# Lane pacing in a fused decoder layer: longer waits in the weight joining, a staging tile for the second output projection, and earlier loads of the norm's gains

## The chip, the cores and the metric

The kernel runs on one core of one Trainium2 chip. A core has several engines that run side by side, each with its own queue of instructions in order: TensorE (PE: matrix products; its weight loads are shown as PEld), VectorE (DVE), ScalarE (ACT), GpSimd (POOL), and SyncE (SP), which here does nothing but issue transfers. Transfers run on 16 DMA engines. The metric is the device time of one execution in microseconds (us); lower is better. Before the change three runs took 1999.65 to 2007.75 us, with a median of 2001.74 us.

## What is computed

One decoder layer on an input x of 2048 rows and 1024 columns, all in float32:

```python
hn = rms_norm(h, mix_pre_g)
proj = hn @ w_in                       # 1024 -> 1792: q, k, v, u
attn_out = sliding_window_attention(q, k, v, attn_sinks, rel_bias)
conv_out = conformer_conv(u, conv_dw, ..., w_conv_pw)
mixed = concatenate([attn_out, conv_out]) @ w_out
h = h + rms_norm(mixed, mix_post_g)
hn = rms_norm(h, ffn_pre_g)
f = (silu(hn @ w_gate) * (hn @ w_up)) @ w_down        # 1024 -> 2816 -> 1024
h = h + rms_norm(f, ffn_post_g)
```

Attention looks 128 positions back. The convolution group is a gated unit, a depthwise convolution with 31 taps, a norm, a swish and a pointwise product with `w_conv_pw`.

## The kernel before

**Precision.** A float32 value is split in a high part, in a format that TensorE takes at full speed, and the low rest, and each product is the sum of three matmuls (`three`, line 108 issues them): high by high, high by low, low by high. A split is an ACT copy for the high part and a subtraction for the low one. `split_w` (lines 128 to 138) does this for weights, with the copy on ACT at line 133 and the subtraction on POOL at line 135 when it takes place beside the early stages; it can also read a low part kept in memory, which is the transfer at line 132.

**Stages.** The rows are cut in four groups of 512, numbered 0 to 3. TensorE goes through these main stages, each of them a Python generator:

- A0 to A3 (7 to 496 us of the span): the input projection of each group, tiles `mm@A`.
- W1 (496 to 579): the output projection of group 1. W0, W2 and W3, the same stage for the other groups, are not main stages but are fed in beside others: W0 beside A3, W2 and W3 beside the main stage G0.
- F0 (579 to 1014): gate and up products of groups 0 and 1. Their operands, made from the normed rows of group 0 and 1, are called H; the first is B11, made by `stage_h_plain`.
- G0 (1014 to about 1325): the down product of these groups, tiles `mm@G`.
- F2 (about 1325 to 1781) and G2 (1781 to 1985): the same for groups 2 and 3.

**Lanes.** Everything else is fed in by lanes. A lane holds a list of generators. Each time the main stage yields a number (its estimate of time passed), every lane gets that number times its rate as credit; it runs its first generator until the credit is spent by what that generator yields. So a larger yield in a side stage lets more main work pass before its next step. Lane `lb` carries attention (B0 to B3, tiles `tr@B`, `p@B`, `sm@B`), `lc` the taps of the convolution (`fc@C`), `ld` (rate 2.0) the joining J and the convolution tails C0 and C1, `lw` W0 (rate 1.7) and later C2, W2, C3, W3 and the norm N3 (1.25), and `lh` the operands of F. `until(name)` runs a lane on, without regard to credit, until that item is done.

A scheduler then orders the instructions of each engine by the priorities that the program gives them and by its own estimate of time. So an edit in a lane may reorder any engine. The transfers are issued in order by SP for the most part, so that one that waits for its buffer holds up those behind it.

**J** (`stage_join`, lines 622 to 650) multiplies the pointwise weight of the convolution with the lower half of the output weight, once, and writes `w_join`, which the W stages read. It loads four double tiles of `w_out` and two of `w_pw` into the single `wx` buffer, splits each on ACT and POOL, and makes eight 128 by 512 results in the single `ct` bank, which the tails use too. After each load it yields 1.5.

**W stages** (`stage_w`, lines 714 to 756). A stage takes eight 128-row pieces of the mixed activations (`mixT`) in four pairs. `load` fetches the two pieces of a pair (line 732) in tiles of the tag `mtag`, `acts` splits them (ACT copy at line 723, DVE subtraction), and for each pair and each half of the columns `block_half` does four products of six matmuls. W0, W2 and W3 yield 5.0 after their first load, and load the next pair at the first half of the present one (n = 0). W1 loads its next pair inside `acts`, at the second half (n = 1), into the two `at` tiles, which attention uses for its output as well.

After the products `norm_w` (lines 758 to 801) squares the sums, loads the norm's gains (`load_gb`, line 705: two tiles of the tag `gb`, of which there are two), scales the rows (`post_scale`, four rows by two halves: eight DVE instructions), adds x, writes `h_scr`, norms again and writes `hn_scr`. The operands of F read `hn_scr` back, turn it on TensorE (`turned`, line 829) and copy it through `gb` tiles as well (`stage_h_plain`, line 849, with a transfer of the tile at line 850 and the split at 852).

The number of buffers per tag that matter here: `wx` 1, `gb` 2, `at` 2, `mb` 2, `fa` 4, `hl` 8.

Of the kernel before, what the change touches and what calls it, by code (L numbers as in the profile page):

```python
# [25 lines left out]
P = 128  # L26
T = 512
NT = S // T
KC = D // P
# [8 lines left out]
def layer_kernel(ctx, tc, x, xT, cols, rows, sinks, relb, onehot, w_in, w_pw, w_out, w_gate, w_up, w_down, out):  # L38
# [10 lines left out]
    def nm(s):  # L49
        uid[0] += 1  # L50
        return f"{s}@{lab[0]}_{uid[0]}"
# [3 lines left out]
    def t_(tag, shape, dt=F32):  # L55
        return sb.tile(list(shape), dt, tag=tag, name=nm(tag), bufs=BUFS[tag])

    def f4(tag, shape=(P, D)):
        return t_(tag, shape)

    def f2(tag, shape=(P, T)):
        return t_(tag, shape)

    def hl(tag):
        return t_(tag, (P, 2, T), F32R)
# [63 lines left out]
    def split_w(raw, tag, low=None, made=False, on_pool=True):  # L129
        w = tag if not isinstance(tag, str) else hl(tag)  # L130
        if made:
            nc.sync.dma_start(w[:, 1].bitcast(F32), low)
        act(w[:, 0], raw, AF.Copy)  # L133
        if not made:
            (ptt if on_pool else vtt)(w[:, 1], raw, w[:, 0].bitcast(F32), ALU.subtract)
            if low is not None:
                (nc.gpsimd if on_pool else nc.sync).dma_start(low, w[:, 1].bitcast(F32))
        return w

    def weight(src, low, made, raw=None, on_pool=True):  # L140
        if raw is None:
            raw = t_("raw", (P, 2, T))
            nc.sync.dma_start(raw, src)
        return [split_w(raw[:, n], "w", low[n], made, on_pool) for n in range(2)]
# [43 lines left out]
    def three(o, pairs, first=True, last=True):  # L188
        n = 3 * len(pairs)
        i = 0  # L190
        for (sh, sl), (mh, ml) in pairs:
            for a, b in ((sh, mh), (sh, ml), (sl, mh)):
                mat(o, a, b, start=first and i == 0, stop=last and i == n - 1)
                i += 1
# [426 lines left out]
    def stage_join():  # L621
        lab[0] = "J0"
        right = []
        for k in range(4):
            raw = f4("wx", (P, 2, T))
            nc.sync.dma_start(raw, w_out[4 + k].rearrange("p (a b) -> p a b", a=2))
            yield 1.5
            for n in range(2):
                lab[0] = "J0"
                right.append(split_w(raw[:, n], "mid" if k < 2 else "chl"))  # L630
            yield 1.5
            lab[0] = "J0"
        for mp in range(2):
            pair_ = t_("yt", (P, 2, 2, T), F32R)
            raw = f4("wx", (P, 2, T))
            nc.sync.dma_start(raw, w_pw[2 * mp : 2 * mp + 2].rearrange("m p t -> p m t"))
            yield 1.5
            lab[0] = "J0"
            left = [split_w(raw[:, m], pair_[:, m]).rearrange("p a (k c) -> p a k c", c=P) for m in range(2)]
            yield 2  # L640
            for m in range(2):
                for n in range(2):
                    lab[0] = "J0"
                    o = ct()
                    three(o, [((left[m][:, 0, k], left[m][:, 1, k]), (right[2 * k + n][:, 0], right[2 * k + n][:, 1])) for k in range(4)])
                    z = f2("fa")
                    act(z, o, AF.Copy, scale=0.5)
                    nc.scalar.dma_start(w_join[2 * mp + m, :, n * T : (n + 1) * T], z)
                    yield 4
                    lab[0] = "J0"  # L650
# [37 lines left out]
    def block_half(acc, units, n, first, L, bank_of, s0=0):  # L688
        cs = slice(n * T, (n + 1) * T)
        for i in range(len(acc)):  # L690
            s = i + s0
            lab[0] = L
            o = bank_of()
            three(o, [((a[s // 4][:, 0, ss(s)], a[s // 4][:, 1, ss(s)]), (w[:, 0], w[:, 1])) for a, w in units])
            if first:
                act(acc[i][:, cs], o, AF.Copy)
            else:
                vtt(acc[i][:, cs], acc[i][:, cs], o, ALU.add)
            yield 0.65 * len(units)

    def load_gb(row):
        gb = []
        for n in range(2):
            t = f2("gb")
            nc.sync.dma_start(t, rows[row, n * T : (n + 1) * T].partition_broadcast(P))
            gb.append(t)
        return gb
# [6 lines left out]
    def stage_w(w, spill, G, atag, htag, mtag, bank_of, norm=None):  # L714
        L = f"W{w}"
        lab[0] = L
        acc = [f4(atag) for _ in range(4)]

        def acts(gi, ms=None):
            aa = []  # L720
            for m in ms or load(gi):
                a = hl(htag)
                act(a[:, 0], m, AF.Copy)  # L723
                vtt(a[:, 1], m, a[:, 0].bitcast(F32), ALU.subtract)
                aa.append([a])
            return aa

        def load(gi):
            ms = []
            for c in range(G * gi, G * gi + G):  # L730
                ms.append(f2(mtag))
                nc.sync.dma_start(ms[-1], mixT[c, :, w * T : (w + 1) * T])
            return ms

        first = load(0)
        if w != 1:
            yield 5.0
            lab[0] = L
        nxt = acts(0, first)
        for gi in range(KC // G):  # L740
            aa = nxt
            for n in range(2):
                lab[0] = L
                if n == 0 and w != 1 and gi + 1 < KC // G:
                    rows_next = load(gi + 1)
                if n == 1 and gi + 1 < KC // G:
                    if w == 1 and G * gi + G == 4:
                        ld.until("C1")
                        lab[0] = L
                    nxt = acts(gi + 1, rows_next if w != 1 else None)  # L750
                src = w_out[2 * gi : 2 * gi + 2] if gi < 2 else w_join[2 * gi - 4 : 2 * gi - 2]
                ws = weight(src[:, :, n * T : (n + 1) * T].rearrange("c p t -> p c t"),
                            lo_out[n, 2 * gi : 2 * gi + 2], w > 0)
                yield from block_half(acc, list(zip(aa, ws)), n, gi == 0, L, bank_of)
        tail = norm_w(w, spill, acc, mtag)
        if norm:
            norm(tail)
        else:
            yield from tail

    def norm_w(w, spill, acc, mtag):
        L = f"W{w}"
        lab[0] = L
        gb = load_gb(0)
        ssq = sm(4)
        for s in range(4):
            act(junk, acc[s], AF.Square, accum_out=ssq[:, s : s + 1])
            yield 0.5
            lab[0] = L
        r = rsqrt(ssq, 4, D, w < 3)  # L770
        yield 3
        lab[0] = L
        ssq2 = sm(4)
        for s in range(4):
            lab[0] = L
            post_scale(acc[s], gb, r[:, s : s + 1])
            r0 = w * T + s * P
            if s == (2 if mtag == "fa" else 0):
                xt = f4("wx")
                nc.sync.dma_start(xt, x[r0 : r0 + P])  # L780
                vtt(acc[s], xt, acc[s], ALU.add)
            else:
                for n in range(2):
                    cs = slice(n * T, (n + 1) * T)
                    xt = f2(mtag if s == 1 or w > 1 else "fa")
                    nc.sync.dma_start(xt, x[r0 : r0 + P, cs])
                    vtt(acc[s][:, cs], xt, acc[s][:, cs], ALU.add)
            nc.sync.dma_start(h_scr[r0 : r0 + P], acc[s])
            act(junk, acc[s], AF.Square, accum_out=ssq2[:, s : s + 1])
            yield 5.0  # L790
        lab[0] = L
        r2 = rsqrt(ssq2, 4, D, w < 3)
        yield 3
        lab[0] = L
        for s in range(4):
            act(acc[s], acc[s], AF.Copy, scale=r2[:, s : s + 1])
            if spill:
                r0 = w * T + s * P
                nc.scalar.dma_start(hn_scr[r0 : r0 + P], acc[s])
        yield 0.1  # L800
        hns[w] = acc
# [484 lines left out]
    def since(lane, name, dt):  # L1286
        return name in lane.done and clk[0] >= lane.done[name] + dt
# [64 lines left out]
    PRE_S0, PRE_S2 = 22, 16  # L1352
    H1, H2, H3, H4 = 0, 4, 7, 11
    NH = 24
    lb = Lane(RB, 0)
    lc = Lane(RC0, LC)
    lw = Lane(RW0, 0)
# [73 lines left out]
    for n, off in (("B11", 0), ("B21", 4)):  # L1431
        lh.add(n + ".0", stage_h_plain(ws, ops, n, off), lambda: since(lw, "W0", NH))
    run(stage_w(1, True, 2, "mid", "hl", "at", mm, norm=lambda g: lh.add("N1", g)))
# [85 lines left out]
```

## Time and profile before

| what | value |
|---|---|
| median of 3 runs | 2001.74 us |
| the profiled execution's own time | 1996.83 us |
| its span in the profile | 1994.7 us |
| TensorE busy | 1939.1 us, 97% of the span |
| VectorE busy | 1490.7 us, 75% |
| ScalarE busy | 971.3 us, 49% |
| GpSimd busy | 332.6 us, 17% |
| moved between memory and core | 452.49 MB, 227 GB/s |

Times are us from the start of the span. In the rows of a timeline stand the start, the length, the engine (SPq is SP's transfer queue), the line of the kernel, the operation, output<-inputs as tile@stage, the shape, and how many such instructions follow one another; in brackets the idle time of the engine before it, and the engine, tile and line whose end released it. Matmuls are pipelined, so that the length of a group is more than what it adds to TensorE's time by the tail of its last matmul. In the rows of a list of stretches stand the stretch, its length, the busy time (and number of instructions) of PE, PEld, DVE, ACT and POOL, the clock granted to TensorE as a share of the full one, the busy share of the DMA engines, and GB/s.

### The profile page before, as it was taken

What the parts mean: (1) busy time and instruction counts of PE and PEld (TensorE: products, weight loads), DVE (VectorE), ACT (ScalarE), POOL (GpSimd) and SP (SyncE); (2) the same over time, 40 slices, a digit from 0 to 9 for tenths busy, and PEclk for the clock granted to TensorE, in tenths of its full rate; (3) what the DMA queues carried; (4) which work ended last, traced back from release to release, by engine and by line L of the source; (5) the groups of instructions that cost most, each with busy time, mean ns of one, the idle gap of its engine ahead of it and who ended that gap; (6) DMA issues with size and microseconds to landing.
All of it is one profiled execution on the core that took longest, in us unless ns stands there. A gap on an engine that the chain in (4) does not pass through costs nothing. (4 is left out here: it accounts for less than half of the span.)

```text
span 1994.7 us, 26920 instructions
## 1 busy us (share of the span) xinstructions
PE 1939.1 (97%) x8730; PEld 1544.5 (77%) x8730; DVE 1490.7 (75%) x2679; ACT 971.3 (49%) x1910; POOL 332.6 (17%) x395
## 2 busy tenths in 40 slices
PE   8999999999899999999999999989999999999998
PEld 7877677677667878878878878778788888888886
DVE  5998997887684899988759985675866665545557
ACT  5355344646566733334355446656644333345443
POOL 5001312241110300000000020002523332311000
PEclk9999999999899999999999999999999999999999
DMA  8886656558759876787477677779844442366654
GB/s 309 266 308 212 205 160 199 183 187 283 247 187 330 288 255 227 238 279 261 157 265 249 228 266 267 234 275 349 310 143 169 169 153 101 125 223 212 210 182 162
DMA packets 234077, 452.49 MB, mean 227 GB/s; under 512 B 23464, under 2 KB 49232, under 8 KB 233936
## 3 DMA queue, kind: packets, MB, share of 16 engines
q1 hardware_dynamic: 212304, 415.11, 61.9%
q10 hardware_dynamic: 19392, 28.32, 3.9%
q0 software_dynamic: 2240, 7.34, 0.9%
q8 instruction: 69, 1.13, 0.2%
q14 instruction: 72, 0.59, 0.1%
HBM read 329.55 MB, written 121.12 MB: 226 GB/s over the span
## 5 line engine op out<-in xcount | busy, mean ns | idle before, releaser
L85 DVE SCALAR_TENSOR_TENSOR fc@C<-glu@C,colt,fc@C 128x512 f32<-128x512 f32 x480 | 369.2, 784 | 2.8
L108 PE MATMUL mm@F<-hl@H,w@F 128*128 128x512 f32 x1056 | 254.7, 391 | 0.0
L108 PE MATMUL mm@G<-hl@G,hl@G 128*128 128x512 f32 x924 | 225.2, 395 | 8.6 <-DVE x@G L85 6.0
L108 PEld LDWEIGHTS mm@F<-hl@H,w@F 128*128 128x128 f32 x1056 | 197.8, 188 | 41.5
L108 PE MATMUL mm@A<-hl@A,w@A 128*128 128x512 f32 x840 | 207.5, 396 | 3.9 <-ACT hl@A L319 1.4
L108 PEld LDWEIGHTS mm@G<-hl@G,hl@G 128*128 128x128 f32 x924 | 172.9, 189 | 47.8 <-ACT gb@H L849 6.2
L811 ACT ACTIVATE w@F<-chl@F 128x512 fp32r<-128x512 f32 x220 | 135.8, 625 | 136.9 <-PE mm@F L108 130.2
L108 PE MATMUL mm@G<-w@G,hl@G 128*128 128x512 f32 x876 | 199.5, 389 | 0.0
L108 PEld LDWEIGHTS mm@G<-w@G,hl@G 128*128 128x128 f32 x876 | 164.4, 188 | 34.2
L108 PEld LDWEIGHTS mm@A<-hl@A,w@A 128*128 128x128 f32 x840 | 155.8, 188 | 43.7 <-issue 4.2
L85 DVE TENSOR_TENSOR w@F<-chl@F,w@F 128x512 fp32r<-128x512 f32 x198 | 144.5, 731 | 39.4 <-ACT w@F L811 39.0
L108 PE MATMUL mm@F<-mid@H,w@F 128*128 128x512 f32 x528 | 133.2, 397 | 3.9 <-ACT mm@F L938 3.9
L108 PE MATMUL mm@F<-ql@H,w@F 128*128 128x512 f32 x528 | 128.2, 391 | 4.6 <-ACT w@F L811 4.6
L108 PE MATMUL mm@F<-p@H,w@F 128*128 128x512 f32 x528 | 130.3, 392 | 0.2 <-ACT at@F L1060 0.2
L108 PE MATMUL mm@F<-x@H,w@F 128*128 128x512 f32 x528 | 125.1, 390 | 0.0
L108 PEld LDWEIGHTS mm@F<-mid@H,w@F 128*128 128x128 f32 x528 | 99.5, 190 | 26.1 <-ACT mm@F L938 5.0
L108 PEld LDWEIGHTS mm@F<-ql@H,w@F 128*128 128x128 f32 x528 | 99.1, 188 | 25.9 <-ACT w@F L811 5.5
L108 PEld LDWEIGHTS mm@F<-p@H,w@F 128*128 128x128 f32 x528 | 99.9, 190 | 21.7 <-ACT at@F L1060 0.8
L108 PEld LDWEIGHTS mm@F<-x@H,w@F 128*128 128x128 f32 x528 | 98.8, 188 | 22.8 <-issue 2.4
L108 PE MATMUL mm@W<-w@W,hl@W 128*128 128x512 f32 x384 | 107.2, 413 | 4.9 <-ACT hl@W L723 3.6
L108 PE MATMUL tr@W<-w@W,ql@W 128*128 128x512 f32 x384 | 98.7, 397 | 4.3 <-ACT ql@W L723 3.4
L133 ACT ACTIVATE w@A<-raw@A 128x512 fp32r<-128x512 f32 x110 | 66.9, 626 | 73.3 <-PE mm@A L108 40.1
(301 smaller groups left out, 3274.7 us busy)
## 6 DMA issues: line engine op xcount, KB each, us to landing
mids<-fa@F SPq DMA_DIRECT2D x154, 256.0 KB, 2.8
raw@A<-w_in SPq DMA_DIRECT2D x55, 512.0 KB, 4.7
w@A<-lo_in SPq DMA_DIRECT2D x84, 256.0 KB, 3.8
fc@G<-mids SPq DMA_DIRECT2D x77, 256.0 KB, 3.4
fa@G<-mids SPq DMA_DIRECT2D x75, 256.0 KB, 4.6
gb@F<-keeps SPq DMA_DIRECT2D x72, 256.0 KB, 4.3
w@W<-lo_out SPq DMA_DIRECT2D x48, 256.0 KB, 4.3
raw@F<-w_gate SPq DMA_DIRECT2D x22, 512.0 KB, 3.4
```

The costliest lines, as they stand in the source:

```text
L85: r = op(*args, **kw)
L108: r = nc.tensor.matmul(*args, **kw)
L133: act(w[:, 0], raw, AF.Copy)
L811: act(w[:, 0], x, AF.Copy)
```

## The change

1. J yields `JL` = 10 in place of 1.5 between each of its six loads and the split of what was loaded.
2. W1 gets one tile `stage` of the tag `mb` (two halves of 512 columns), through which all its pieces of `mixT` pass, and loads the next pair at n = 0 as the other W stages do. The call that waits for the tail C1 stands ahead of that load.
3. W2 and W3 yield 8.0 in place of 5.0 after their first load; W0 keeps 5.0.
4. W2 and W3 load the norm's gains right after their first rows and hand them to `norm_w`; W0 and W1 load them in `norm_w` as before.

```diff
--- before.py
+++ after.py
@@ -624,7 +624,7 @@
         for k in range(4):
             raw = f4("wx", (P, 2, T))
             nc.sync.dma_start(raw, w_out[4 + k].rearrange("p (a b) -> p a b", a=2))
-            yield 1.5
+            yield JL
             for n in range(2):
                 lab[0] = "J0"
                 right.append(split_w(raw[:, n], "mid" if k < 2 else "chl"))
@@ -634,7 +634,7 @@
             pair_ = t_("yt", (P, 2, 2, T), F32R)
             raw = f4("wx", (P, 2, T))
             nc.sync.dma_start(raw, w_pw[2 * mp : 2 * mp + 2].rearrange("m p t -> p m t"))
-            yield 1.5
+            yield JL
             lab[0] = "J0"
             left = [split_w(raw[:, m], pair_[:, m]).rearrange("p a (k c) -> p a k c", c=P) for m in range(2)]
             yield 2
@@ -725,43 +725,46 @@
                 aa.append([a])
             return aa
 
+        stage = t_("mb", (P, 2, T)) if w == 1 else None
+
         def load(gi):
             ms = []
             for c in range(G * gi, G * gi + G):
-                ms.append(f2(mtag))
+                ms.append(stage[:, c % 2] if w == 1 else f2(mtag))
                 nc.sync.dma_start(ms[-1], mixT[c, :, w * T : (w + 1) * T])
             return ms
 
         first = load(0)
+        gb = load_gb(0) if w > 1 else None
         if w != 1:
-            yield 5.0
+            yield 5.0 if w == 0 else 8.0
             lab[0] = L
         nxt = acts(0, first)
         for gi in range(KC // G):
             aa = nxt
             for n in range(2):
                 lab[0] = L
-                if n == 0 and w != 1 and gi + 1 < KC // G:
-                    rows_next = load(gi + 1)
-                if n == 1 and gi + 1 < KC // G:
+                if n == 0 and gi + 1 < KC // G:
                     if w == 1 and G * gi + G == 4:
                         ld.until("C1")
                         lab[0] = L
-                    nxt = acts(gi + 1, rows_next if w != 1 else None)
+                    rows_next = load(gi + 1)
+                if n == 1 and gi + 1 < KC // G:
+                    nxt = acts(gi + 1, rows_next)
                 src = w_out[2 * gi : 2 * gi + 2] if gi < 2 else w_join[2 * gi - 4 : 2 * gi - 2]
                 ws = weight(src[:, :, n * T : (n + 1) * T].rearrange("c p t -> p c t"),
                             lo_out[n, 2 * gi : 2 * gi + 2], w > 0)
                 yield from block_half(acc, list(zip(aa, ws)), n, gi == 0, L, bank_of)
-        tail = norm_w(w, spill, acc, mtag)
+        tail = norm_w(w, spill, acc, mtag, gb)
         if norm:
             norm(tail)
         else:
             yield from tail
 
-    def norm_w(w, spill, acc, mtag):
+    def norm_w(w, spill, acc, mtag, gb):
         L = f"W{w}"
         lab[0] = L
-        gb = load_gb(0)
+        gb = gb or load_gb(0)
         ssq = sm(4)
         for s in range(4):
             act(junk, acc[s], AF.Square, accum_out=ssq[:, s : s + 1])
@@ -1352,6 +1355,7 @@
     PRE_S0, PRE_S2 = 22, 16
     H1, H2, H3, H4 = 0, 4, 7, 11
     NH = 24
+    JL = 10
     lb = Lane(RB, 0)
     lc = Lane(RC0, LC)
     lw = Lane(RW0, 0)
```

## The prediction

> **What bounds the kernel now.** I read the page's first and fourth part, then busy time by stage, then the waits of TensorE, then the timelines around the longest of them.
>
> ```profile
> span 1994.7 us, 26920 instructions
> PE 1939.1 (97%) x8730; PEld 1544.5 (77%) x8730; DVE 1490.7 (75%) x2679; ACT 971.3 (49%) x1910; POOL 332.6 (17%) x395
> PE 27%; DVE 1%; DMA 0%; ACT 0%; issue 0%; DVEq 0%; SPq 0%; ACTq 0%
> ```
>
> The next rows are stretches of the span: length, busy time of each engine, granted clock, DMA share.
>
> ```profile
> 200.00:240.00 40.00, 35.31 (x169) 25.41 (x166) 39.75 (x72) 16.16 (x43) 14.76 (x10) 0.96 0.58 197
> 300.00:496.00 196.00, 194.15 (x894) 140.75 (x893) 159.37 (x323) 103.76 (x238) 53.81 (x80) 1.00 0.66 211
> 496.00:579.00 83.00, 73.75 (x359) 51.12 (x358) 62.23 (x173) 46.81 (x114) 9.78 (x17) 0.94 0.68 228
> 520.00:560.00 40.00, 31.84 (x160) 20.97 (x159) 30.34 (x87) 19.74 (x58) 4.16 (x4) 0.91 0.65 200
> 579.00:1014.00 435.00, 428.88 (x1898) 349.71 (x1897) 344.20 (x546) 200.93 (x371) 26.02 (x39) 1.00 0.74 250
> 1310.00:1330.00 20.00, 16.48 (x65) 13.55 (x66) 14.89 (x27) 10.96 (x21) 0.00 (x0) 0.83 1.01 358
> 1325.00:1985.00 660.00, 656.10 (x2907) 542.03 (x2905) 413.50 (x651) 307.27 (x566) 149.77 (x125) 1.00 0.57 196
> ```
>
> TensorE is the bound: 97% of the span, and no engine but it has a real share of the chain that ended last. Only 1994.7 − 1939.1 = 55.6 us of it are idle, and they are bunched: 9.3 us in the 83 us of W1 (496 to 579), 4.7 us in 40 us at J's splits (200 to 240), 3.5 us in 20 us at W3's norm. The change does not alter the 8,600-odd matmuls, so a gain can come only from these holes, from the half clock that follows them, and from the cost of switching between sorts of matmul.
>
> **W1's rows through a staging tile, half a block earlier.** The waits of TensorE from 496 to 579 (engine, line, tile, who ended it, us, times, longest), then the places themselves on TensorE, ScalarE and the SP queue:
>
> ```profile
> PE mm@W L108 <- ACT hl@W L723: 3.6, 2, 2.5
> PE tr@B L108 <- ACT p@B L502: 3.3, 1, 3.3
> PE mm@W L108 <- DVE mid@W L85: 1.2, 1, 1.2
> PE tr@B L501 <- ACT gb@H L849: 1.0, 1, 1.0
> ```
>
> ```profile
> 547.04 3.33 PE L108 MATMUL mm@W<-w@W,hl@W 128*128 128x512 f32 x12 [2.52 <-ACT hl@W L723]
> 546.35 0.63 ACT L723 ACTIVATE hl@W<-at@W 128x512 fp32r<-128x512 f32 x1 [2.99 <-DMA at@W<-mixT]
> 541.33 0.40 SPq L732 DMA_DIRECT2D at@W<-mixT  x1
> ```
>
> ScalarE stood 2.99 us for a row whose load was issued at 541.33: it landed 5.0 us later, and the split, its low part and the product followed. It shared the "at" tiles with attention's output, and was asked for only where it was needed. In the order of the changed kernel these loads stand on the SP queue far ahead, the first pair beside the last projection; and twelve of W1's products stand between attention's transposes and the products that use them, which covers the 3.3 us. I let all four waits go: 3.6 + 3.3 + 1.2 + 1.0 = 9.1 us, and with them the half clock, 40 us × (1 − 0.91) = 3.6 us. That is −12.7.
>
> What was hidden behind these holes must be hidden elsewhere. In W1 before, all eight transposes of H's first operand ran; in the new order three do, and the other five come among F0's first products. Their chain is long on ScalarE and VectorE:
>
> ```profile
> 540.47 0.69 ACT L849 ACTIVATE gb@H<-tr@H,colt 128x512 f32<-128x512 f32 x1 [0.43 <-PE tr@H L829]
> 556.22 0.69 ACT L849 ACTIVATE gb@H<-tr@H,colt 128x512 f32<-128x512 f32 x1 [1.84 <-DVE x@H L85]
> 559.77 0.69 DVE L85 TENSOR_TENSOR x@H<-gb@H,x@H 128x512 fp32r<-128x512 f32 x1
> 574.80 4.36 PE L108 MATMUL mm@W<-w@W,hl@W 128*128 128x512 f32 x18
> ```
>
> Four operands took 540.47 to 560.46, 5.0 us each, while twelve products take 12 × 4.36/18 = 2.9 us. Bounds: nothing, if they fill it; 4 × (5.0 − 2.9) = 8.4 us for four operands, if nothing does. I take +3, nearer to nothing, because by the new order attention's matmuls and W1's last blocks stand ahead of the first two of these operands and attention's alone ahead of the rest; if the cover is there for none, the 8.4 is due. The early loads carry a price too: in the single staging tile a load waits for the low part (VectorE) of the row before, with weight loads behind it on SP. Weights stand a block ahead there, so nothing; without that cover one landing, 5.0 us.
>
> **W2's and W3's gains loaded with the first rows; their yield 5.0 to 8.0.** At W3's norm (TensorE's wait, then who made it):
>
> ```profile
> 1313.52 13.77 PE L108 MATMUL mm@G<-hl@G,hl@G 128*128 128x512 f32 x52 [6.02 <-DVE x@G L85]
> 1300.83 2.74 DVE L85 SCALAR_TENSOR_TENSOR mid@W<-mid@W,sm@W,gb@W 128x512 f32<-128x512 f32 x4 [3.26 <-DMA gb@W<-rows]
> 1292.44 0.32 SPq L1151 DMA_DIRECT2D fa@G<-mids  x1
> 1297.02 0.33 SPq L705 DMA_DIRECT2D gb@W<-rows  x1
> 1297.44 0.38 SPq L1155 DMA_DIRECT2D mb@G<-w_down  x1
> 1301.48 0.63 ACT L811 ACTIVATE hl@G<-mb@G 128x512 fp32r<-128x512 f32 x1 [4.12 <-DMA mb@G<-w_down]
> ```
>
> The gains' load stood at the head of SP from 1292.8 to 1297.0, until H's tiles gave back its buffers; VectorE then waited 3.26 us for it, did eight scalings in a row, and G's weight, queued behind on SP, came 4.12 us late to ScalarE. TensorE stood 6.02 us, and ran at 0.83 of its clock over the 20 us that follow: 20 × 0.17 = 3.4 us. With the load ahead of W3's products both go: −9.4. What is late next: the eight scalings (4 in 2.74 us, so 5.5 us of VectorE) now run before the tiles of H that the next product needs (B11.2), whose ScalarE copies need those same two buffers and have G's splits behind them in order. Between 0 and 5.5 us come back, 6.0 at most if the old stall forms anew; I take +4, nearer the upper end, because G's operand must still pass the same two engines. W2's gains already stood on SP well ahead, and its yield of 8.0 moves only splits that wait for nothing: 0.
>
> A rule that could cut either way stands in the Trainium skill, "TensorE: Matmul & The Clock Gate", Part 1: an idle window of about 3.4 us halves the clock, and a busy one of that length brings it back. Here the 6.02 us hole was followed by the loss above, which agrees. By the rule W1's three holes of 1.0 to 2.5 us would cost no clock; were none of the 0.91 theirs, the term would be −9.1 and the sum −12.4.
>
> **J with 10 in place of 1.5 between loads and splits.** Each of the six loads gets 8.5/2.0 = 4.25 us of the planner's clock more at the lane's rate of 2.0, so J ends some 6 × 4.25 = 25 us later, and C0's and C1's tails and W0 after it crowd into the last projection. What J cost at its old place:
>
> ```profile
> 227.04 1.28 PE L108 MATMUL tr@B<-kz,ql@A 64*128 64x256 f32 x12 [3.60 <-DVE sm@B L460]
> 215.58 5.68 DVE L85 SCALAR_TENSOR_TENSOR fc@C<-glu@C,colt,fc@C 128x512 f32<-128x512 f32 x6
> 214.32 0.74 DVE L85 SCALAR_TENSOR_TENSOR fc@C<-glu@C,colt,fc@C 128x512 f32<-128x512 f32 x1
> 215.07 2.99 POOL L135 TENSOR_TENSOR chl@J<-wx@J,chl@J 128x512 fp32r<-128x512 f32 x2 [1.87 <-ACT chl@J L133]
>   DMA wx@J<-w_out: 8.6, 2
>   DMA wx@J<-w_pw: 5.8, 1
> ```
>
> The last two rows are J's tile: idle of the engine that waited for its loads, which the added yields take from ScalarE. VectorE was full there (39.75 of 40 us), and a tap took 0.95 us beside J's subtracts in place of 0.74. TensorE lost 3.60 us and 40 × 0.04 = 1.6 us of clock. With J gone the taps still fill VectorE, so I give back half, −2.6; and in the last projection, where VectorE is busy 159.37 of 196 us and TensorE idle for 1.85, I charge the same 5.2 once, since all of it now meets there: +2.6 net. Bounds: −5.2 if it costs nothing there; +18 as in the third rival.
>
> Why a subtract on GpSimd slows a tap: the Trainium skill, "GPSIMD Engine Reference", says that GpSimd shares its SBUF interfaces with VectorE, with contention for VectorE instructions of two SBUF inputs, as a tap has. The 0.95 beside 0.74 agrees; the rule speaks against the change, since moved subtracts slow whatever they meet.
>
> **Switches.** The new order has fewer changes between attention's 256-wide matmuls and 512-wide ones, 105 for 122.
>
> ```profile
> 499.08 0.38 PE L108 MATMUL tr@B<-kz,ql@A 64*128 64x256 f32 x1
> 499.39 0.49 PE L108 MATMUL mm@W<-w@W,hl@W 128*128 128x512 f32 x1
> 499.81 0.38 PE L108 MATMUL tr@B<-kz,ql@A 64*128 64x256 f32 x1
> 562.70 0.98 PE L108 MATMUL tr@B<-kz,ql@A 64*128 64x256 f32 x12
> ```
>
> One of each alternating takes 0.73 us (499.81 − 499.08); in runs 0.98/12 + 4.36/18 = 0.32. Half of 17 switches, 8.5 round trips × 0.41 = −3.5.
>
> **Sum.** −12.7 + 3 − 9.4 + 4 + 2.6 − 3.5 = −16.0 us. The profiled execution took 1996.83 us (span 1994.7 and 2.1 around it), so 1980.8; the median of the runs is 4.9 us above it, so the forecast stands at 2001.7 − 16.0 = 1985.7. F0, F2 and G2, whose order stays but for the first products, keep their time.
>
> **The rivals.** *The holes move* (they are put back at F0's first products and at W3's norm): +3 becomes 8.4 with its half clock of 1.7 (half of 3.4), +4 becomes 6.0 and 3.4, so −16.0 + 7.1 + 5.4 = −3.5: 1998. For it: both chains pass the same ScalarE, VectorE and two buffers; against it: the loads that ended both waits are gone. *The yields do nothing, the rest works*: J's and the switch terms are 0, so −15.1, in the forecast's range. The likelier form of "does not do what it says" is that W3 alone or W1 alone gains: −9.7 − 0.9 or −5.4 − 0.9, 1991 to 1995. *Slower: the tails crowd on one bank.* C0's and C1's 16 uses of the single "ct" bank and J's 8 come closer together; each turn not covered costs about the 0.98 us of the buffer wait in W1. All 24 make 23.5 us for the 2.6 charged, and 0.04 of the clock over some 150 us of the projection 6 us: −16.0 + 20.9 + 6 = +10.9, 2012.6. It is slower than before from 24 × 16/26.9, some 15 uncovered turns, on. For it: crowding in a stage that has 1.85 us idle; against it: TensorE has attention and projection products to put between.
>
> **Chances.** Forecast (gain over 10 us) 0.50, moved holes and half-working forms 0.32, crowding 0.18, of which two thirds slower by over 0.5%. 0.5% is 10 us, about what a measurement of this kernel tells from no change. Faster 0.50, same 0.36, slower 0.14. The range runs from all returns nil (−12.7 − 9.4 − 5.2 − 3.5 = −30.8, cut to −28) to +6 within the crowding: 1974 to 2008. The forecast's own range is 1974 to 1991.
>
> **What would show it.** Right: no wait for hl@W from 496 to 579, clock 1.00 there; no 6 us wait at W3's norm; the tap at 0.74 near 215. Wrong: TensorE waiting for x@H at F0's start, for x@G again at about 1300, or for ct tiles between 300 and 500; then the sum loses the return terms first, and J's term next.

## The result and the profile after

The changed kernel takes 1993.27 us in the median of 7 runs (1986.81 to 1994.27), beside 2000.74 us for 7 runs of the kernel before (1998.09 to 2007.75). The ratio is 0.9951, with a 95% interval of 0.9932 to 0.9970: about 9.8 us (6.0 to 13.6) less of 2001.74. The forecast was 1985.7 us within 1974 to 2008, 16 us less. The direction came, and about half (by the medians) to three fifths (by the ratio) of the gain.

The profiled execution of the changed kernel has a span of 1991.2 us, only 3.5 less than that of before; why these two show less than the runs is told in the last section. Here are its span and engines, and the stretches that were shown of before (stretch, length, busy time of PE, PEld, DVE, ACT and POOL, granted clock, DMA share, GB/s).

```profile
span 1991.2 us, 26908 instructions
PE 1939.0 (97%) x8730; PEld 1546.6 (78%) x8730; DVE 1484.8 (75%) x2679; ACT 970.2 (49%) x1910; POOL 322.4 (16%) x395
```

```profile
200.00:240.00 40.00, 35.32 (x164) 25.31 (x164) 39.75 (x70) 16.73 (x43) 14.70 (x11) 0.91 0.60 204
300.00:496.00 196.00, 188.18 (x877) 137.04 (x877) 149.15 (x318) 105.31 (x238) 47.82 (x80) 0.98 0.61 196
496.00:579.00 83.00, 82.06 (x401) 58.79 (x400) 71.78 (x184) 47.76 (x116) 7.60 (x18) 1.00 0.70 236
579.00:1014.00 435.00, 426.36 (x1886) 345.36 (x1884) 343.69 (x556) 201.19 (x372) 29.46 (x39) 1.00 0.75 253
1310.00:1330.00 20.00, 20.00 (x92) 16.57 (x91) 17.96 (x38) 14.84 (x31) 0.00 (x0) 1.00 1.05 376
```

Two holes closed, as forecast: W1's stretch (496 to 579) went from 73.75 us busy at a clock of 0.94 to 82.06 at 1.00, and the 20 us after W3's norm from 16.48 at 0.83 to 20.00 at 1.00. Two opened: the last projection (300 to 496) went from 194.15 us busy to 188.18 and from a clock of 1.00 to 0.98, and F0 from 428.88 to 426.36. And J's spot (200 to 240) did not change at all, 35.31 to 35.32, but for a lower clock.

The waits of TensorE in three stretches of the changed kernel (who waited, for whom, us, times, longest): from 300 to 500, in F0 (567 to 1015), and in G0 (1014 to 1348).

```profile
PE mm@W L108 <- ACT hl@W L723: 5.9, 3, 3.9
PE mm@W L108 <- ACT x@W L696: 1.9, 1, 1.9
```

```profile
PE mm@F L108 <- ACT w@F L814: 3.8, 2, 2.1
PE mm@F L108 <- ACT mm@F L941: 2.6, 3, 1.9
PE mm@F L108 <- DVE gb@F L85: 1.6, 2, 0.8
PE mm@F L108 <- DVE x@H L85: 0.9, 1, 0.9
```

```profile
PE tr@W L108 <- ACT ql@W L723: 4.9, 2, 3.4
PE tr@W L108 <- DVE mid@W L85: 4.1, 1, 4.1
```

All the waits for hl@W, the split rows of W0 and W1, stand beside the last projection now, in W0; before they stood in W1. The wait for x@G is gone, and one of 4.1 us stands earlier in the same stage:

```profile
1262.63 3.78 PE L108 MATMUL tr@W<-w@W,ql@W 128*128 128x512 f32 x8 [4.06 <-DVE mid@W L85]
```

### The profile page after: what moved, and what is told of

Read it like the earlier page. It is cut to its first block, busy times and chain, and to the rows that moved or that the text cites. A ratio compares the mean times of both kernels' runs of the same rounds, so it can differ in the third digit from the quotient of the medians.

```text
span 1991.2 us, 26908 instructions
## 1 busy us (share of the span) xinstructions
PE 1939.0 (97%) x8730; PEld 1546.6 (78%) x8730; DVE 1484.8 (75%) x2679; ACT 970.2 (49%) x1910; POOL 322.4 (16%) x395
## 4 chain that ended last, share of the span: by engine, by line
PE 47%; DVE 8%; DMA 8%; issue 3%; ACT 1%; POOL 0%; SPq 0%; DVEq 0%; ACTq 0%; POOLq 0%
PE mm@F L108 24%; PE mm@G L108 18%; PE tr@W L108 4%; DMA gb@F<-keeps 2%; DVE fc@C L85 2%; DVE w@F L85 1%; DVE chl@F L85 1%; DVE fa@F L85 1%; DMA fc@G<-w_down 1%; DMA mids<-fa@F 1%; DMA mixT<-fc@C 1%; DMA td<-fc@G 1%; DMA at@W<-mixT 1%; DVE mid@W L85 0%; DMA chl@F<-w_up 0%
## 5 line engine op out<-in xcount | busy, mean ns | idle before, releaser
L108 PE MATMUL mm@W<-w@W,hl@W 128*128 128x512 f32 x384 | 103.1, 406 | 7.8 <-ACT hl@W L723 5.9
```

The costliest lines, as they stand in the source:

```text
L108: r = nc.tensor.matmul(*args, **kw)
```

## The experiments

All ratios below are to the kernel before, from runs on the same chip, with their 95% intervals; a difference "in us" is the ratio times 2001.74. The idle time of TensorE by stage is the length of the stage less its busy time, in the stretch between the stage's own borders (the projection from 300 us on). It is from one profiled execution each.

| kernel | ratio | in us | proj. | W1 | F0 | G0 | F2 |
|---|---|---|---|---|---|---|---|
| before | 1 | 0 | 1.9 | 9.3 | 6.1 | 14.5 | 3.9 |
| changed | 0.9951 (0.9932 to 0.9970) | −9.8 | 7.8 | 0.0 | 9.6 | 13.3 | 0.9 |
| J alone | 1.0011 (0.9994 to 1.0029) | +2.2 | 8.2 | 7.8 | 6.9 | 15.1 | 3.2 |
| W1's staging alone | 0.9982 (0.9966 to 0.9999) | −3.6 | 1.6 | 5.2 | 10.0 | 13.0 | 5.2 |
| W2 and W3 alone | 0.9976 (0.9960 to 0.9991) | −4.8 | 2.0 | 11.4 | 7.4 | 8.7 | 6.3 |
| changed, less J | 0.9949 (0.9930 to 0.9969) | −10.2 | 1.8 | 4.9 | 9.9 | 13.3 | 1.1 |
| changed, less W1's staging | 0.9988 (0.9975 to 1.0001) | −2.4 | 8.2 | 8.7 | 5.6 | 12.2 | 6.6 |
| changed, less the yield of 8 | 0.9973 (0.9963 to 0.9984) | −5.4 | 8.1 | 0.0 | 9.3 | 11.4 | 5.5 |
| changed, less the early gains | 0.9993 (0.9980 to 1.0006) | −1.4 | 8.1 | 0.0 | 11.4 | 18.8 | 1.2 |
| changed, W0's yield 7 | 0.9962 (0.9949 to 0.9975) | −7.6 | 6.8 | 0.0 | 14.8 | 9.8 | 5.2 |
| less J, operand later | 0.9952 (0.9938 to 0.9967) | −9.6 | 1.7 | 0.0 | 10.8 | 10.2 | 5.9 |
| less J, copy on VectorE | 0.9944 (0.9924 to 0.9964) | −11.2 | 1.7 | 6.4 | 6.7 | 11.3 | 5.0 |
| changed, copy on VectorE | 0.9962 (0.9949 to 0.9976) | −7.6 | 7.2 | 0.0 | 13.0 | 8.9 | 5.3 |
| less J, operand later, copy on VectorE | 0.9933 (0.9914 to 0.9951) | −13.4 | 2.0 | 0.0 | 15.1 | 10.2 | 6.2 |

### Each part alone, and the change without J

**J alone** (the kernel before with the longer yields, `JL` = 10, after each of J's six loads):

```diff
-            yield 1.5
+            yield JL
```

> J's longer yields alone, the rest as before. Theory 1 (J made the new waits of the last projection): TensorE waits about 3.9 us for W0's first split near 358 and 3 to 4 us more for W0 before 440, against 1.85 us of waits from 300 to 496 before, and loses up to 3.4 us of clock there; W1 and W3's norm keep their holes (9 and 6 us); the time is 2 to 8 us above before. Rival (those waits came with W1's early loads, which stand on the SP queue beside the last projection): 300 to 496 keeps under 3 us of waits, and the time is between 4 us below before and the same, the fewer switches being all that is left.

Measured: 2.2 us above before (−1.2 to +5.8). The waits that the changed kernel has from 300 to 500 are here too, with no other part of the change:

```profile
PE mm@W L108 <- ACT hl@W L723: 6.4, 3, 3.9
PE mm@W L108 <- ACT x@W L696: 1.9, 1, 1.9
```

So J's yields make them; W1's early loads don't. How they do is seen in the changed kernel, on ScalarE and TensorE:

```profile
354.08 0.39 ACT L479 ACTIVATE p@B<-p@B,sm@B 128x128 f32<-128x128 f32 x1
357.16 0.62 ACT L723 ACTIVATE hl@W<-fa@W 128x512 fp32r<-128x512 f32 x1
357.83 0.79 PE L108 MATMUL mm@W<-w@W,hl@W 128*128 128x512 f32 x1 [3.89 <-ACT hl@W L723]
```

W0's split (357.16) stands on ScalarE behind eight exponentials of attention that begin at 354.08, and W0's first product waits 3.89 us for it, with products of the projection in order behind. In the kernel before, the first two splits of W0 (348.29) stood ahead of the exponentials (350.17). The time came within the theory's range, though its interval reaches into the rival's; the place is settled, the size is not.

**W1's staging alone:**

```diff
+        stage = t_("mb", (P, 2, T)) if w == 1 else None
...
-                if n == 0 and w != 1 and gi + 1 < KC // G:
+                if n == 0 and gi + 1 < KC // G:
```

> The staging tile and the earlier loads of W1 alone. Theory 1: no wait over 1 us from 496 to the start of F0, clock 1.00 there, the stage 14 us shorter; F0 takes over some 5 to 8 us of moved attention work and operand turns; the time is 6 to 11 us below before. Rival (F0 gives it all back, since ScalarE's chain for its operands only moved): waits in F0 rise by 6 us or more and the time is within 4 us of before.

Measured: 3.6 us below before (6.8 to 0.2 below), less than theory 1 wanted and at the edge of the rival's range. The waits of W1 (497 to 575) begin with this, and the places on TensorE and ScalarE are:

```profile
PE tr@H L832 <- ACT gb@H L852: 4.3, 2, 3.5
```

```profile
553.17 0.66 PE L832 MATMUL tr@H<-ident,fa@H 128*128 128x128 f32 x4 [3.54 <-ACT gb@H L852]
```

```profile
548.76 0.39 ACT L479 ACTIVATE p@B<-p@B,sm@B 128x128 f32<-128x128 f32 x1
552.46 0.67 ACT L852 ACTIVATE gb@H<-tr@H,colt 128x512 f32<-128x512 f32 x1
```

The wait for hl@W is gone from W1. In its place TensorE waits for the copy of F0's operand out of its bank, which stands behind eight such exponentials (548.76 on; the copy at 552.46). And F0's idle time rises from 6.1 to 10.0 us.

**W2's and W3's part alone** (yield 8.0, gains with the first rows):

> W2's and W3's yield of 8.0 and their earlier gains alone. Theory 1: the 6.0 us wait at W3's norm and the half clock behind it are gone (9.4 us), and a wait of 3 to 5 us with a half clock of 1.7 to 3.4 stands at about 1262 for W3's last pieces; the time is 1 to 5 us below before. Rival (the wait at 1262 came with the other parts): no wait over 2 us from 1200 to 1300, 8 to 10 us below before.

Measured: 4.8 us below before (8.0 to 1.8 below), as theory 1 had it, but not on its reason: the wait near 1262 is not there, G0's idle falls from 14.5 to 8.7, and the norm's wait is 1.20 us in place of 6.02:

```profile
1309.45 5.88 PE L108 MATMUL mm@G<-hl@G,hl@G 128*128 128x512 f32 x22 [1.20 <-DVE x@G L85]
```

What came back stood in F2 (3.9 to 6.3), and in part in W1, where this kernel's order is that of before and its idle differs by 2 us all the same.

**The changed kernel with J's yields at 1.5:**

> The changed kernel with J's yields put back to 1.5. Theory 1: the waits of the last projection fall back to about 2 us and those of the second part stay; the time is 4 to 9 us below the changed kernel, 11 to 17 below before. Rival (the longer yields pay for their waits by fewer switches between kinds of matmul): within 3 us of the changed kernel, 5 to 10 below before.

Measured: 10.2 us below before (14.0 to 6.2 below), the same as the changed kernel, which is the rival's time. The waits of the projection go (7.8 to 1.8), and W1's come back (0.0 to 4.9), the 4.3 us for gb@H of W1's staging alone. Neither theory had named that second place. In the full change J costs about what it saves.

### Why J pays for itself, and what the other two parts are worth

J's first product comes 33 us later than before, W0's first one 8 us later (357.83 for 350.05), and the first turn of F0's operand, which is read from W0's normed rows, 14 us later than in the changed kernel less J (559.48 for 545.50). It then stands among W1's last products. Its copies meet eight exponentials on ScalarE there too, but TensorE has work of W1 and of attention meanwhile and waits for none of them:

```profile
560.12 0.69 ACT L852 ACTIVATE gb@H<-tr@H,colt 128x512 f32<-128x512 f32 x1 [2.53 <-PE tr@H L832]
560.70 0.39 ACT L479 ACTIVATE p@B<-p@B,sm@B 128x128 f32<-128x128 f32 x1
565.91 0.67 ACT L852 ACTIVATE gb@H<-tr@H,colt 128x512 f32<-128x512 f32 x1
```

If that lateness is all that J does for W1, letting in the operand later by itself must do the same without the waits of the projection. `NH` says how long after W0 it is let in:

```diff
-    NH = 24
-    JL = 10
+    NH = 28
+    JL = 1.5
```

> J's yields at 1.5, the other parts kept, and the first operand of F0 let in 4 of the planner's us later (NH 28 in place of 24). Theory 2 (J's longer yields help W1 only because W0, and with it this operand, comes later, out of the way of attention's eight exponentials on ScalarE): the waits for gb@H in W1 (0.8 and 3.5 us) and the half clocks there go, as in the changed kernel, and the last projection keeps its 2 us of waits; the time is 3 to 7 us below both the changed kernel and the one with J's yields put back. Rival (the turns only wait in F0 in place of W1): F0's waits grow by as much and the time stays within 2 us of them.

Measured: 9.6 us below before (12.4 to 6.6 below). The rows are W1's and F0's stretches, by this kernel's own borders:

```profile
498.21:560.23 62.02, 62.02 (x298) 45.21 (x299) 47.10 (x129) 34.52 (x92) 5.62 (x11) 0.97 0.65 210
560.23:1011.81 451.58, 440.83 (x1960) 356.55 (x1961) 357.74 (x586) 210.86 (x388) 29.50 (x40) 0.99 0.75 250
```

W1 has no idle time and the projection keeps its 1.7 us: the place is as theory 2 says. But the time is that of the kernel it came from, as the rival says, and F0 has 10.8 us of idle time for 9.9. W1 with 62 us has handed its attention work and the operand's turns to F0, which is 9.5 us longer (451.58, against 442.09 with NH 24).

**The changed kernel with W0's first yield at 7.0:**

```diff
-            yield 5.0 if w == 0 else 8.0
+            yield 7.0 if w == 0 else 8.0
```

> The changed kernel with W0's first yield at 7.0 in place of 5.0, so that products of the last projection stand ahead of W0's first one, behind whose split attention's eight exponentials ran on ScalarE. Theory 1: the 3.9 us wait at W0's first product goes, and the half clock of up to 3.4 us with it; the time is 3 to 7 us below the changed kernel. Rival (W0's rows themselves are late): the wait stands at the new place, the time within 2 us of the changed kernel.

Measured: 7.6 us below before (10.2 to 5.0 below); no gain over the changed kernel. The waits for hl@W in the projection fall from 5.9 to 1.0 us:

```profile
PE mm@W L108 <- ACT hl@W L723: 1.0, 1, 1.0
PE mm@W L108 <- DVE x@W L85: 1.5, 1, 1.5
```

The places on ScalarE and TensorE show why:

```profile
358.31 0.61 ACT L723 ACTIVATE hl@W<-fa@W 128x512 fp32r<-128x512 f32 x1
360.49 4.41 PE L108 MATMUL mm@W<-w@W,hl@W 128*128 128x512 f32 x18
```

The split still stands behind the eight exponentials (355.21 on), but TensorE has ten products of the projection ahead of W0's first one. So the wait takes both: a late split, and an order on TensorE with nothing to cover it. Four other waits take the place, and the stage's idle falls by 1 us in all, while F0's rises from 9.6 to 14.8. Theory 1 was right about the wait and wrong about the time.

**The changed kernel with W2's and W3's yield at 5.0:**

> The changed kernel with W2's and W3's yield back at 5.0. Theory 1: no large wait at W3's norm either way, and the wait of about 4 us near 1262 stays, since it is that of C3's last store; within 2 us of the changed kernel. Rival (the yield of 8.0 moved the products that stood ahead of that wait): it shrinks below 2 us, the time 3 to 6 us below the changed kernel.

Measured: 5.4 us below before (7.4 to 3.2 below), 4.4 above the changed kernel. The two intervals overlap (0.9963 to 0.9984 and 0.9932 to 0.9970), so theory 1's 2 us stays possible; the rival's gain doesn't. G0 and F2 waited so:

```profile
PE mm@G L108 <- DVE x@G L85: 1.6, 1, 1.6
PE tr@W L108 <- DVE mid@W L85: 1.2, 2, 0.8
```

```profile
PE mm@F L108 <- ACT mm@F L941: 5.2, 5, 2.2
```

The 4.1 us wait at 1262 is gone with the yield, as the rival had it; but F2 waits 5.2 us for the seeding of its banks on ScalarE, where the changed kernel waits 0.9. In the table the two go together: where G0 has its wait near 1262 (4.1 to 5.5 us), in the changed kernel and in those less J and less the early gains, F2 has about 1 us of idle time; everywhere else it has 3 to 7. The wait at 1262 itself is that of a row which W3 reads back from memory right after C3 stored it. The transfer queue of the changed kernel stood for that store:

```profile
SPq L734 <- DMA mixT<-fc@C: 6.8, 2, 4.7
```

Why the order of G0 decides F2's waits so far behind it was not tried.

**The changed kernel with the gains loaded in the norm, as before:**

> The changed kernel with W2's and W3's gains loaded in the norm, as before. Theory 1: the wait of about 6 us at W3's norm comes back with its half clock, 5 to 9 us above the changed kernel. Rival (the yield of 8.0 removed it): no such wait, the time within 2 us of the changed kernel.

Measured: 1.4 us below before (−4.0 to +1.2), 8.4 above the changed kernel, as theory 1 had it. The wait at the norm comes back with less than half its size, and others grow:

```profile
PE mm@G L108 <- ACT hl@G L814: 3.9, 2, 2.9
PE mm@G L108 <- DVE x@G L85: 2.7, 1, 2.7
```

### W1's staging in company, and ScalarE's exponentials

**The changed kernel with W1's rows loaded as before:**

> The changed kernel with W1's rows loaded as before (J's yields, W2's and W3's parts kept). Theory 3 (the staging is worth more with the longer yields of J than alone, because with them H's operand is out of W1's way): W1 waits 7 to 9 us again and loses 5 to 8 us of clock, and the time is 6 to 12 us above the changed kernel. Rival (the staging is worth what it showed alone, 0.2 in 100): up to 5 us above the changed kernel.

Measured: 2.4 us below before (5.0 below to 0.2 above), so 7.4 above the changed kernel: theory 3's range, though the two intervals (0.9975 to 1.0001 and 0.9932 to 0.9970) leave the rival's 5 us possible. W1, by its own borders, and its main wait:

```profile
500.22:585.54 85.32, 76.67 (x361) 54.92 (x360) 71.17 (x189) 47.52 (x125) 8.68 (x17) 0.88 0.68 219
```

```profile
PE mm@W L108 <- ACT hl@W L723: 7.8, 2, 4.5
```

Here W1 waits 8.7 us and has a clock of 0.88, so that the staging closes more than it does alone.

**The first copy of F0's operand on VectorE**, in the kernel less J, in the changed one, and in the one less J with the operand later:

```diff
-            act(u, b, AF.Copy, scale=g_ffn[:, k + off : k + off + 1])
+            if ws[0]:
+                act(u, b, AF.Copy, scale=g_ffn[:, k + off : k + off + 1])
+            else:
+                vts(u, b, g_ffn[:, k + off : k + off + 1], 0.0, ALU.mult, ALU.add)
```

> J's yields at 1.5, the other parts kept, and the first copy of each tile of H's operand for groups 0 and 1 made by VectorE instead of ScalarE, so that it no longer stands behind attention's eight exponentials. Theory 4 (those exponentials, in order on ScalarE, make the 3.5 us wait of TensorE for gb@H in W1): that wait falls below 1 us, with the half clock of 1.7 us; the time is 2 to 6 us below the same kernel with the copy on ScalarE. Rival (the split behind the copy, still on ScalarE, or the two gb buffers hold the chain): a wait of 2 us or more stays in W1, or F0's waits grow, and the time is within 2 us of it.

> The changed kernel with the same copy on VectorE. Theory 4: no wait for it stood in W1, so W1 keeps its 0 us of waits and the time stays within 2 us of the changed kernel. Rival (the operand's chain on ScalarE also feeds the waits in F0, 9.5 us): F0's waits fall by 3 us or more and the time by 3 to 6 us.

> J's yields at 1.5, the other parts kept, H's operand let in 4 of the planner's us later (NH 28) and its first copy on VectorE. Theory 4: no wait for it stood in W1, so within 2 us of the same kernel with the copy on ScalarE. Rival (as for the run before): F0's waits fall from 10.7 us by 3 or more, and the time by 3 to 6 us, to some 13 us below before.

Measured: less J, −11.2 us (1.0 below the same with the copy on ScalarE, which these intervals can't tell from nothing). W1's waits are now these:

```profile
PE tr@H L832 <- DVE gb@H L85: 3.0, 2, 1.8
PE tr@B L108 <- ACT p@B L502: 2.8, 1, 2.8
```

The 3.5 us wait shrank to 1.8, but a second one and attention's own waits joined it, 6.4 us in all for 4.9. The exponentials held the copy; without them the chain behind it holds as much. That is the rival of theory 4. On the changed kernel the copy on VectorE gave −7.6 us, with F0's idle up from 9.6 to 13.0; the rival there, that F0 would wait less, fell. With the operand later it gave −13.4 us (17.2 to 9.8 below), the lowest ratio of all and in the rival's range, but F0's idle rose to 15.1, so not for the rival's reason. Its 6 runs were granted 0.993 of the clock in the mean, the 23 of before beside them 0.988: about 10 us of half clock less, which is most of the gain. Its interval (0.9914 to 0.9951) overlaps that of the changed kernel (0.9932 to 0.9970), so it isn't shown to be faster; nothing else beat the change.

## Why the prediction was right, and where its sum was off

The kernel is faster, and the runs show two of the forecast's reasons: W1's staging and the early gains. Without either, the time is back within noise of before (0.9988 and 0.9993, both above the changed kernel's interval). Without J's part nothing changes. The tile and the earlier load of the staging weren't tried apart.

The size is another matter, 9.8 us for 16. The table sets the terms of the sum beside the two profiled executions: by how much TensorE's idle time changed in each place, and by how much what half clock cost it there. That cost is its busy time in stretches of a quarter of a us, times what the granted clock lacks of 1.

| term | forecast | idle | half clock |
|---|---|---|---|
| W1's waits and clock | −12.7 | −9.3 | −4.7 |
| return in F0 | +3 | +3.5 | 0.0 |
| J, at 200 to 240 and in the projection | −2.6 + 5.2 | +5.9 | +4.2 |
| W3's norm and its return, in G0 | −9.4 + 4 | −1.2 | +3.8 |
| F2 | 0 | −3.0 | −1.7 |
| elsewhere | 0 | +0.7 | +1.7 |

Idle time and half clock make −3.4 and +3.3 together. The rest, −3.4 us, is busy time at full clock, 1925.9 us before and 1922.5 after; the forecast had −3.5 there, for switches. These are single executions, and the half clock in them is a draw (last section).

- *TensorE's 55.6 us of holes are what can be won*: held as a bound. The idle time of the span is still 1991.2 − 1939.0 = 52.2 us, since as much opened in new places as closed in the old ones.
- *W1's staging, −12.7 for the waits and the clock*: held in place. All four waits went, the clock is 1.00, and 9.3 + 0.06 × 79 = 14 us of idle time and clock are gone. But they aren't the staging's alone. Without J's yields it leaves 4.9 us of idle time and a clock of 0.93 in W1. The term took the lateness of F0's operand to be the staging's doing, and J does that: its first turn stands at 539.77 before, at 545.87 with the staging alone and at 553.70 with J alone. So the staging is worth 3.6 us alone and 7.4 in company, for a forecast of 9.7, which the intervals of the second leave possible.
- *The 3.6 us of clock in that term*: right in size. In the kernel before the clock was halved from the end of the 3.3 us wait on, in the stretch below, and from 504.5 to 508, where TensorE didn't wait. It was not halved behind the holes of 1.0 to 2.5 us, of which there are four and not three. So none of the loss was theirs; but the 3.3 us wait went too, and the term stays at −12.7.

```profile
532.00:539.00 7.00, 6.04 (x23) 2.41 (x25) 6.30 (x19) 1.91 (x5) 0.81 (x1) 0.51 0.34 112
```

- *"+3" for what returns in F0*: 3.5 us of idle time came. But only 0.9 is a wait for x@H at F0's first products, where the prediction looked; the others are for weights and banks further on, so that the number is in part luck. Wherever W1's idle time falls to nothing, F0's rises by 3 to 9 us over the 6.1 of before. The work that stood in W1's holes, attention's above all, was not free.
- *W3's norm, −9.4 + 4 = −5.4*: the part alone gave −4.8 us, near the sum, but both terms differ from what the traces show. The eight scalings start at 1290.00 in place of 1300.83, and the wait went:

```profile
1290.00 2.74 DVE L85 SCALAR_TENSOR_TENSOR mid@W<-mid@W,sm@W,gb@W 128x512 f32<-128x512 f32 x4
```

  The 3.4 us of clock in the −9.4 are too much. In the kernel before, half clock stood for 7 us, and TensorE was idle in the first half of them, so that only the second half cost anything, 3.5 × 0.50 = 1.8 us:

```profile
1310.00:1313.50 3.50, 0.00 (x0) 0.01 (x1) 3.50 (x7) 3.50 (x7) 0.00 (x0) 0.55 0.94 280
1313.50:1317.00 3.50, 3.48 (x8) 2.81 (x9) 3.47 (x6) 0.10 (x2) 0.00 (x0) 0.50 0.95 347
```

  The "+4" was to be the scalings in the way of the next operand; with the part alone 1.20 us is left of that wait. What the changed kernel has instead is the 4.06 us at 1262 with 2.7 us of half clock; no wait of that size stands there in a kernel that lacks the staging or the yields of 8.0. So its G0 is no shorter than before (333.15 us for 331.60), and F2 is (421.40 for 426.55). "W2's yield: 0" is not settled: without the yields of 8.0 the changed kernel is 4.4 us slower, with intervals that overlap, and F2, which the prediction took to keep its time, has 4.6 us more of idle time.
- *J, "give back half" at 227*: wrong, and the term most off. All of J's splits but the last pair stayed within 2 us of where they were. The next rows are the changed kernel's subtracts on GpSimd, its taps, the wait of TensorE, and J's products with their first and last start:

```profile
223.80 3.07 POOL L135 TENSOR_TENSOR yt@J<-wx@J,yt@J 128x512 fp32r<-128x512 f32 x2 [5.26 <-ACT yt@J L133]
216.02 5.73 DVE L85 SCALAR_TENSOR_TENSOR fc@C<-glu@C,colt,fc@C 128x512 f32<-128x512 f32 x6
227.53 1.86 PE L108 MATMUL tr@B<-kz,ql@A 64*128 64x256 f32 x12 [3.72 <-DVE sm@B L460]
```

```profile
L108 PE MATMUL ct@J<-mid@J,yt@J x48: 387/393/504, 256.2 to 329.5; 128*128 128x512 f32 x48
```

  The subtract stands at 223.80 (before 222.97), a tap takes 5.73/6 = 0.96 us, the wait is 3.72 us: all as before. What moved are the last two splits (266 to 289), the products, from 223 to 256, and W0 behind them. "The same 5.2 once in the last projection" was too low: 5.9 us of idle time and 2.8 of half clock, 8.7 in all. That +2.6 is near the +2.2 of J alone is luck: two errors, set off by busy time that the new order saves (next point). In company J takes waits and half clock from W1, and its cost comes to nothing.
- *Switches, −3.5*: the size agrees, the cause isn't isolated. Seven kernels have J's longer yields and seven have not. TensorE's busy time at full clock is 1918.4 to 1925.4 us in the former and 1923.2 to 1928.2 in the latter, 3.7 us less in the mean, and up to 620 us the changes between 256-wide and 512-wide matmuls number 144 to 152 and 158 to 162. No run has fewer switches and nothing else.
- *The rivals*: "the holes move" is what happened to more than a third of the gain, but not at the places named: W0 beside the projection and the wait at 1262 took it, and W3's norm did not. "The tails crowd on one bank" did not come: no wait for the ct bank stands among those of 300 to 500.

## What to carry to other kernels

When a wait is to be closed in a stage that is full of side work, price what fills the hole and where it goes, and not only the wait that ends it. Here the staging alone closed less than half of W1's idle time, since another wait came up behind the first, and what the parts are worth depends on which others are there. Before costing an effect at the old place of a step that is "moved", look in the new order for which of its instructions move; here the yields moved J's products and left most of its splits. Count half clock only where TensorE works; what falls into the wait itself costs nothing more. On an engine that works in order, look for the block of eight small instructions (here attention's exponentials, 3 us) and for what a shift places behind it, and then whether TensorE has other work for that time.

## What the runs showed of the hardware

The same wait can cost one or two lengths of half clock. TensorE waited 3.60 us at 227 in the profile of before and 3.72 us in that of the changed kernel; the stretch around it is, in the kernel before and then in the changed one,

```profile
224.00:236.00 12.00, 8.92 (x39) 7.11 (x40) 11.86 (x33) 2.54 (x7) 2.39 (x2) 0.86 0.53 197
```

```profile
224.00:236.00 12.00, 8.47 (x32) 6.80 (x33) 11.86 (x34) 3.52 (x8) 2.88 (x2) 0.72 0.60 213
```

with 12 × 0.14 = 1.7 and 12 × 0.28 = 3.4 us of clock missing. From 229 to 231 and from 228 to 232 the clock is 0.50, so this is half clock for 3.4 us and for 6.8. The Trainium skill, "TensorE: Matmul & The Clock Gate", Part 1, says that the window of 3.4 us by which the gate decides runs free of the kernel, and calls the cost run-variable, which agrees. Each of the two profiled executions has seven such stretches, so one execution is a draw: the 29 runs of the kernel before on one chip lay between 1998.93 and 2013.78 us. The 81 runs of that kernel on three chips were granted 0.988 to 0.989 of the clock in the mean, its profiled execution 0.991; the 7 runs of the changed kernel 0.990, its profiled one 0.989. So the two spans differ by 3.5 us where the runs differ by 7.5 in the median, and a price in clock is good to about 1.7 us for each wait.

The length of the wait does not decide it alone. In the changed kernel this wait of 2.38 us had 3.4 us of half clock behind it (4 × 0.43 / 0.50), and one of 1.94 us at 642.11 as much; the wait of 2.52 us at 547.04 in the kernel before had none. So the rule of about 3.4 us that the prediction puts beside its price does not hold for the single waits of these traces:

```profile
31.75 0.91 PE L307 MATMUL ct@A<-ident,gb@A 128*128 128x128 f32 x4 [2.38 <-DVE gb@A L85]
32.00:36.00 4.00, 4.00 (x13) 3.17 (x12) 2.59 (x8) 2.27 (x4) 1.71 (x5) 0.57 0.84 271
```

The clock also fell where TensorE did not wait. At the start of W1 attention's 64-row matmuls alternate one by one with products. The stretch 500 to 520 of the kernel less J with the copy on VectorE is busy throughout and has a clock of 0.74 (0.91 in the kernel before); in the changed kernel, where they alternate as well, it has 1.00:

```profile
500.00:520.00 20.00, 20.00 (x65) 12.47 (x64) 10.12 (x32) 10.25 (x16) 2.27 (x4) 0.74 0.75 269
```

```profile
500.00:520.00 20.00, 20.00 (x84) 13.53 (x84) 16.40 (x43) 13.90 (x23) 4.13 (x12) 1.00 1.03 376
```

What makes it fall there was not tried. The 0.74 costs 20 × 0.26 = 5.2 us, as much as a wait of that length.
